# First projection of layer 0 begun on half of scale and shift; each pair's scatter tied behind the next pair's last up product

## The chip, the cores and the metric

The program runs on one core of a Trainium2 chip. The metric is the device time of one execution in microseconds; the time of a kernel is the median of several runs. The engines named below are TensorE (PE, its weight loads PEld), VectorE (DVE), ScalarE (ACT), GpSimd (POOL) and SyncE (SP), whose queue issues nearly all weight transfers.

## The reference

Two layers of a streaming encoder, 256 frames of 1024 features, in float32. Every sub-layer normalises x, multiplies by 1 + scale and adds shift; scale, shift and a gate come from a conditioning vector c by a matrix product.

```
c_act = silu(c)
sh1, sc1, g1, sh2, sc2, g2 = split(c_act @ w_mod[layer] + b_mod[layer], 6)
h = rmsnorm(x, norm_g) * (1 + sc1) + sh1
layer 0:  q, k, v, f = split(h @ w_in)            # 1024, 1024, 1024, 16 columns
          cum = cumsum(log_sigmoid(f + b_f));  scores = q k / 8 + cum_t - cum_s, causal softmax
layer 1:  latent attention on a shared k/v made from layer 0's output
x = x + g1 * (attention(h) @ w_o)
h = rmsnorm(x, ffn_norm_g) * (1 + sc2) + sh2
x = x + g2 * sum over 16 experts of  combine_e * ((silu(h Wg_e) * (h Wu_e)) Wd_e)   # 2 experts of a frame
out = rmsnorm(x, final_norm_g)
```

## The kernel before

**Weights.** All weights flow through one planned list, `stream`. `plan` appends a piece of mostly 1 MB (L91), `issue` (L238) starts its transfer from SP's queue as soon as one of the ten ring buffers `w` (or a named spare buffer) is free, and `done`/`drop` (L275 to L288) free it and issue the next. The list's order is the order of arrival: the four pieces of scale `sc1_0`, the four of shift `sh1_0` (L185), the forget-gate columns `wf` (L187), and then the twelve pieces of `w_in` (four head groups g, each q, k and v, L189), each followed by one piece of another modulation vector (`g1_0`, `sc2_0`, `sh2_0`; `weave`, L174).

**Modulation.** `mods` (L302) multiplies such pieces with c: those named in `ONPE` on PE (L321), into PSUM bank 6, the others on DVE (L327, L329), two instructions a piece, tied behind the last instruction of the first `turn` (`state["turned"]`). When all four pieces are in, `fin_col` (L457) brings the vector into columns: for `sc1_0` and `sh1_0` by 32 small products each (L464), then two DVE additions (L468, L470).

**Start of layer 0.** x is normalised to `xn`, `turn` (L548) transposes it on PE with feature k of every eighth column together, `leave` (L566) applies scale and shift on the way out of PSUM and splits the result into a high and a low part (`h2`). Every product of this part is three fp32r products (`mm3`, L521: high by high, high by low, low by high); weights are split likewise by `split` (L498), the high part on ACT (L517), the low part on POOL or DVE (L518). The f product (L1075 to L1080) stands first; its result goes through a chain on DVE and ACT (L1083 to L1088) into two rows of q and k. `proj_a` (L1090) makes q, k and v of one head group, 48 products each; `attention` (L643) runs the groups and puts scores, softmax and the value products between them.

**Experts.** `moe` (L747) gathers frames per expert into 64 slots with one-hot products (`fetch`, L869) and walks eight pairs of experts (L976): 64 recorded products for gate and up (`wide`, L899), SiLU (L985), `act` = silu(gate) * up * weight on DVE (L996), transposes of it (L1003), copies `aT` (L1006, L1007), 32 products down in two column halves (L1018), and `yb`, `yh` (L1031 to L1034) as the scaled result. `scatter(i - 1)` (L907, L911) adds the previous pair's `yh` into the output rows in PSUM by eight products; `slots(i + 1)` (L880) makes the next pair's one-hot matrix. Pair OV = 4 is special: its branch for overflowing experts stands behind its gate products, with scatter(3) ahead of it. The last pair scatters half by half (L1044).

**Order.** Every engine runs its instructions in a fixed order. That order is not that of the program text: a planner, which simulates the program on a time line of its own, orders each engine's queue when the kernel is built. `tc.issue_after(x)` forbids it to put the instructions inside ahead of x. So scatter(i - 1), written behind up of pair i (L997), stands for most pairs between the gate products of pair i.

Of the kernel before, what the change touches and what calls it, by code (L numbers as in the profile page):

```python
# [22 lines left out]
F32 = mybir.dt.float32  # L23
# [4 lines left out]
ALU = mybir.AluOpType  # L28
# [18 lines left out]
ONPE = ('sc1_0', 'sh1_0', 'sc2_0', 'sh_kv', 'sh1_1', 'g2_0', 'sc2_1', 'g2_1')  # L47
# [26 lines left out]
def trunk_kernel(ctx, tc, A, out):  # L74
# [217 lines left out]
    nc.gpsimd.memset(bcast, 0.0)  # L292

# [8 lines left out]
    def mods():  # L302
        while state["used"] < len(stream) and stream[state["used"]][0][0] == "mod":
# [5 lines left out]
            if j == 0:  # L309
                macc[name] = bank(MB)[:, 0:256] if name in ONPE else big.tile([128, D], F32, name="macc", bufs=2)  # L310
# [5 lines left out]
            for kk in range(2):  # L316
                k = 2 * j + kk
                if name in ONPE:
                    with later(name, j):
                        for q in range(4):  # L320
                            PE.matmul(acc[32 * q:32 * q + 32, :], cact[:, k:k + 1].to_broadcast([128, 32]),  # L321
                                      w[:, kk, 256 * q:256 * q + 256], start=k == 0, stop=k == 7)
# [9 lines left out]
            if j == 3:  # L332
# [124 lines left out]
    def fin_col(name, bias, gain=None):  # L457
        rows = mod_rows(name)
        r_ = cst.tile([128, 8], F32, name="c_" + name)
        if name in ("sc1_0", "sh1_0"):  # L460
            at = bank(MB)[:, 0:8]
            for k in range(8):
                for q in range(4):
                    PE.matmul(at[32 * q:32 * q + 32, k:k + 1], rows[:, k::8], pick[:, q:q + 1], start=True, stop=True)  # L464
        else:
            nc.gpsimd.dma_start(r_, rows[0:128:32, :].rearrange("p (j k) -> p j k", k=8))
            at = r_
        V.tensor_tensor(r_, at, bias, op=ALU.add)  # L468
# [278 lines left out]
    def moe(l, G, sh, acc):  # L747
# [143 lines left out]
        def wide(nm, i, b):  # L891
            ps = bank(b)
            for c, (k0, nk) in enumerate(wide_rows(nm, l, i)):
# [7 lines left out]
                if i == 0 and nm == "g":  # L901
                    after[5] = last
                for e in range(2):
                    done((nm, l, i, c, e))
            return ps

# [69 lines left out]
        for i in range(E // 2):  # L976
# [20 lines left out]
            if i and i != OV:  # L997
                scatter(i - 1)
# [13 lines left out]
            for p, (c0, n) in enumerate(cols):  # L1012
# [15 lines left out]
                if p == 0 and i < E // 2 - 1:  # L1028
                    slots(i + 1, 5)
# [25 lines left out]
    finish_at["sc1_0"] = lambda: fin_col("sc1_0", bcol[0][:, 1, :], pk("ga"))  # L1055
    finish_at["sh1_0"] = lambda: fin_col("sh1_0", bcol[0][:, 0, :])
# [14 lines left out]
    turn(xn, 8, 8, [(h2p, M["sc1_0"], M["sh1_0"], True)], (0, 1, 2, 3))  # L1071
    state["turned"] = state["left"]

    pf = bank(6)
    for c in range(2):  # L1075
        wfs = split(get("wf")[:, 4 * c:4 * c + 4, :], "wf")
        for kk in range(4):
            k = 4 * c + kk
            mm3(pf[0:96, 0:256], [w_[:, kk, :] for w_ in wfs], [h2[:, j, k, :] for j in range(2)], k == 0, k == 7)
    done("wf")  # L1080
# [9 lines left out]
    def proj_a(g, part, qkv):  # L1090
        if part == 0:
# [6 lines left out]
            for j, dst, scl in ((0, qa, HD ** -0.5), (1, ka, 1.0)):  # L1098
                ps = ring_bank()
# [10 lines left out]
            return qa, ka, v  # L1110
        ps = ring_bank().rearrange("p (t n) -> p t n", t=T)
# [278 lines left out]
```

## Time and profile before

| | |
|---|---|
| time, three runs | 857.45 us median (856.47 to 857.65) |
| profiled execution, its own time | 856.38 us |
| its span in the trace | 854.3 us |
| busy in the span | PE 767.0 (90%), DVE 376.0 (44%), ACT 266.6 (31%), POOL 166.2 (19%) |
| transfers | 296.32 MB, mean 347 GB/s; SP's queue 90.8% of 16 DMA engines' span |

The 2.1 us between span and time lie outside the trace. Layer 0's attention runs from the start to 187 us, its experts to 450, layer 1's attention to 600, its experts to the end.

### The profile page before, as it was taken

What the parts mean: (1) busy time and instruction counts of PE and PEld (TensorE: products, weight loads), DVE (VectorE), ACT (ScalarE), POOL (GpSimd) and SP (SyncE); (2) the same over time, 40 slices, a digit from 0 to 9 for tenths busy, and PEclk for the clock granted to TensorE, in tenths of its full rate; (3) what the DMA queues carried; (4) which work ended last, traced back from release to release, by engine and by line L of the source; (5) the groups of instructions that cost most, each with busy time, mean ns of one, the idle gap of its engine ahead of it and who ended that gap; (6) DMA issues with size and microseconds to landing.
All of it is one profiled execution on the core that took longest, in us unless ns stands there. A gap on an engine that the chain in (4) does not pass through costs nothing.

```text
span 854.3 us, 11932 instructions
## 1 busy us (share of the span) xinstructions
PE 767.0 (90%) x4522; PEld 441.9 (52%) x4522; DVE 376.0 (44%) x831; ACT 266.6 (31%) x578; POOL 166.2 (19%) x151
## 2 busy tenths in 40 slices
PE   4678999998999999899978798999799999999994
PEld 2477888765344343243327666777533534434332
DVE  2389599977112211221238949665712321122112
ACT  2346456534101011010127555765511110111002
POOL 1273567320000000000007755321100000000000
PEclk9699999999999999999998999999799999999998
DMA  9997897899999999999997769768789999999992
GB/s 347 383 376 272 275 347 261 315 380 392 414 397 394 417 402 403 418 407 403 414 397 270 231 226 362 293 222 273 269 292 402 402 374 413 367 393 398 402 392 82
DMA packets 102855, 296.32 MB, mean 347 GB/s; under 512 B 6992, under 2 KB 26624, under 8 KB 90496
## 3 DMA queue, kind: packets, MB, share of 16 engines
q1 hardware_dynamic: 101968, 293.79, 90.8%
q10 hardware_dynamic: 288, 1.05, 0.3%
q8 instruction: 39, 0.64, 0.3%
q0 software_dynamic: 528, 0.59, 0.2%
q14 instruction: 32, 0.26, 0.1%
HBM read 294.30 MB, written 1.05 MB: 346 GB/s over the span
## 4 chain that ended last, share of the span: by engine, by line
issue 28%; PE 23%; DVE 5%; DMA 2%; ACT 1%; POOLq 0%; POOL 0%; SPq 0%; another core or an unknown queue 0%; DVEq 0%; ACTq 0%
PE b L899 6%; PE b L1018 4%; PE b L522 2%; PE b L523 2%; PE b L524 2%; DVE macc L329 1%; DMA fg<-in_final_norm_g_dram 1%; PE b L911 1%; PE b L631 1%; DMA w<-in_w_mod_dram 1%; DVE wl L518 1%; DMA w<-in_exp_w_gate_dram 1%; PE b L321 1%; PE b L557 1%; PE b L593 1%
## 5 line engine op out<-in xcount | busy, mean ns | idle before, releaser
L899 PE MATMUL b<-w,XG 128*64 128x512 f32 x1024 | 239.0, 595 | 0.6 <-PEq L917 0.6
L518 POOL TENSOR_TENSOR wl<-w,wh 128x512 fp32r<-128x512 f32 (+3 forms) x90 | 132.4, 1487 | 354.0 <-ACT wh L517 350.5
L899 PEld LDWEIGHTS b<-w,XG 128*64 128x64 f32 x1024 | 78.2, 137 | 140.8 <-issue 135.3
L1018 PE MATMUL b<-w,aT 128*64 128x512 f32 (+1 forms) x528 | 125.8, 585 | 3.7 <-ACT aT L1006 3.7
L996 DVE SCALAR_TENSOR_TENSOR act<-sg,rcs,b 128x512 f32<-128x512 f32 x16 | 12.0, 747 | 211.3 <-PE b L899 211.3
L517 ACT ACTIVATE wh<-w 128x512 fp32r<-128x512 f32 (+3 forms) x136 | 76.6, 587 | 63.3 <-PE b L524 22.7
L1018 PEld LDWEIGHTS b<-w,aT 128*64 128x64 f32 x528 | 38.2, 136 | 66.0 <-issue 56.2
L329 DVE SCALAR_TENSOR_TENSOR macc<-w,cact,macc 128x1024 f32<-128x1024 f32 x42 | 63.6, 1513 | 1.2 <-DMA w<-in_w_mod_dram 0.7
L1033 ACT ACTIVATE yh<-yb 128x512 fp32r<-128x512 f32 x31 | 19.6, 631 | 113.2 <-DVE yb L1031 113.2
L518 DVE TENSOR_TENSOR wl<-w,wh 128x512 fp32r<-128x512 f32 (+2 forms) x46 | 44.3, 973 | 19.8 <-ACT wh L517 19.7
L1031 DVE TENSOR_TENSOR yb<-b,g 128x512 f32<-128x512 f32 (+1 forms) x33 | 22.2, 674 | 64.1 <-PE b L1018 64.1
L985 ACT ACTIVATE sg<-b 128x512 f32<-128x512 f32 x16 | 9.6, 598 | 119.9 <-PE b L899 119.9
L539 POOL TENSOR_TENSOR rs<-rs,mhalf 128x1 f32<-128x1 f32 (+1 forms) x9 | 5.4, 602 | 206.6 <-DVE rs L538 206.6
L321 PE MATMUL b<-w,cact 128*32 128x256 f32 x512 | 39.9, 418 | 6.0 <-DMA w<-in_w_mod_dram 5.7
L524 PE MATMUL b<-h,wl 128*128 128x256 f32 (+1 forms) x136 | 40.5, 299 | 4.7 <-DVE wl L518 4.3
L522 PE MATMUL b<-h,wh 128*128 128x256 f32 (+1 forms) x136 | 40.3, 300 | 3.5 <-ACT h L579 3.5
L1006 ACT ACTIVATE aT<-b 128x256 f32<-128x256 f32 x16 | 6.1, 384 | 117.1 <-PE b L1003 117.1
L869 PEld LDWEIGHTS b<-P,xs 128*128 128x128 f32 x256 | 34.4, 203 | 15.2 <-DVE XG L875 6.5
L869 PE MATMUL b<-P,xs 128*128 128x256 f32 x256 | 39.3, 304 | 1.6 <-DVE P L834 1.6
L523 PE MATMUL b<-h,wh 128*128 128x256 f32 (+1 forms) x136 | 39.5, 292 | 0.0
L911 PE MATMUL b<-yh,PT 128*128 128x512 f32 x112 | 34.4, 422 | 2.1 <-ACT yh L1033 2.1
L523 PE MATMUL b<-wl,h 128*128 128x256 f32 (+1 forms) x96 | 30.0, 316 | 2.9 <-POOL wl L518 2.4
(296 smaller groups left out, 1208.8 us busy)
## 6 DMA issues: line engine op xcount, KB each, us to landing
w<-in_exp_w_down_dram SPq DMA_DIRECT2D x50, 1024.0 KB, 12.5
w<-in_w_mod_dram SPq DMA_DIRECT2D x48, 1024.0 KB, 8.9
w<-in_exp_w_gate_dram SPq DMA_DIRECT2D x48, 1024.0 KB, 12.8
w<-in_exp_w_up_dram SPq DMA_DIRECT2D x48, 1024.0 KB, 13.0
w<-in_a_w_in_dram SPq DMA_DIRECT2D x12, 1024.0 KB, 12.4
w<-in_exp_w_gate_dram SPq DMA_DIRECT2D x42, 256.0 KB, 7.2
w<-in_exp_w_up_dram SPq DMA_DIRECT2D x40, 256.0 KB, 5.9
w<-in_kv_w_mod_dram SPq DMA_DIRECT2D x8, 1024.0 KB, 7.0
```

Source lines behind the costliest of these rows:

```text
L321: PE.matmul(acc[32 * q:32 * q + 32, :], cact[:, k:k + 1].to_broadcast([128, 32]), w[:, kk, 256 * q:256 * q + 256], start=k == 0, stop=k == 7)
L329: V.scalar_tensor_tensor(acc, w[:, kk, :], cact[:, k:k + 1], acc, op0=ALU.mult, op1=ALU.add)
L517: SC.activation(hi, src, AF.Copy)
L518: lo_eng.tensor_tensor(lo, src, hi.bitcast(F32), op=ALU.subtract)
L522: PE.matmul(ps, l[0], r_[0], start=start, stop=False)
L523: PE.matmul(ps, l[0], r_[1], start=False, stop=False)
L524: PE.matmul(ps, l[1], r_[0], start=False, stop=stop)
L869: at = PE.matmul(ps[:, 256 * kk:256 * kk + 256], xs[n % 2, n // 2][:, 128 * k:128 * k + 128], P[g][:, n // 2].rearrange("p e s -> p (e s)" ...
L899: last = PE.matmul(ps[64 * e:64 * e + 64, :], XG[i // 2, k // 4][:, k % 4, o:o + 64], ws[e][:, kk, :], start=k == 0, stop=k == 7).ins
L911: PE.matmul(acc[t, half], PT[i][:, t, :], yh[:, j, 512 * half:512 * half + 512], start=False, stop=False)
L1018: at = PE.matmul(py[64 * e:64 * e + 64, 0:n], aT[:, k, 64 * e:64 * e + 64], ws[e][:, k, :], start=k == 0, stop=k == 3).ins
L1031: V.tensor_tensor(yb[:, 0:n], py[:, 0:n], M[f"g2_{l}"][:, cs_], op=ALU.mult)
```

## The change

There are two parts. In the first, scale and shift of the first sub-layer are fetched and finished in halves of 512 features (`sc1_0a`, `sh1_0a`, then `sc1_0b`, `sh1_0b`), in two 1 MB pieces each. h2 is made in two halves (`turn_half`), with 128 neighbouring features in a block; w_in and wf are read in the matching order, q, k and v of group 0 and wf in half pieces (0.5 MB, wf 0.2 MB) that stand between the second half's modulation pieces. The products of the first half of the features (`half_qk`, `half_v`, `half_f`) are written ahead of the second half's `turn_half(1)`; the sums stay open in PSUM banks 4, 5, 7 and 0. `fin_half` replaces `fin_col` for these vectors: bias and gain are laid out by rows beforehand (`halfrows`, three small DMAs on POOL's queue, in a `macc` buffer), and one product with `pick` turns the row into columns. In the second part, scatter(i - 1) is tied behind the last up product of pair i; in pairs 0 and 4, which have no scatter there, slots(i + 1) takes that place.

```diff
-ONPE = ('sc1_0', 'sh1_0', 'sc2_0', 'sh_kv', 'sh1_1', 'g2_0', 'sc2_1', 'g2_1')
+HALVES = ('sc1_0a', 'sh1_0a', 'sc1_0b', 'sh1_0b')
+ONPE = HALVES + ('sc2_0', 'sh_kv', 'sh1_1', 'g2_0', 'sc2_1', 'g2_1')
...
-    for it in mod_unit("sc1_0", W0, D) + mod_unit("sh1_0", W0, 0):
+    def mod_half(name, c0):
+        r = W0.rearrange("(p k) n -> p k n", k=8)
+        return [(("mod", name, j), r[:, 4 * j:4 * j + 4, c0:c0 + D // 2]) for j in range(2)]
+
+    win = A["a_w_in"][0].rearrange("(k p) n -> p k n", p=128)
+    wff = A["w_f"].rearrange("p (k n) -> (p k) n", k=8).rearrange("(k p) n -> p k n", p=128)
+    def in_half(j, c):
+        return ("in", 0, j, c), win[:, 4 * c:4 * c + 4, j * D:j * D + 256]
+    scb, shb = mod_half("sc1_0b", D + D // 2), mod_half("sh1_0b", D // 2)
+    for it in (mod_half("sc1_0a", D) + mod_half("sh1_0a", 0)
+               + [in_half(0, 0), scb[0], in_half(1, 0), scb[1], shb[0], in_half(2, 0), shb[1], (("wf", 0), wff[:, 0:4]),
+                  (("wf", 1), wff[:, 4:8])]):
         plan(*it)
-    plan("wf", A["w_f"].rearrange("p (k n) -> p k n", k=8))
-    win = A["a_w_in"][0].rearrange("(p k) n -> p k n", k=8)
-    main = [(("in", g, j), win[:, :, j * D + 256 * g:j * D + 256 * g + 256]) for g in range(4) for j in range(3)]
+    main = [in_half(j, 1) for j in range(3)]
+    main += [(("in", g, j), win[:, :, j * D + 256 * g:j * D + 256 * g + 256]) for g in range(1, 4) for j in range(3)]
...
+    def fin_half(name, c, gain):
+        rows = wk.tile([128, 128], F32, name="mrows", tag="t2", bufs=3)
+        V.tensor_tensor(rows, macc.pop(name), halfrows[:, 2 * gain + c], op=ALU.add)
+        if gain:
+            V.scalar_tensor_tensor(rows, rows, 1.0, halfrows[:, 4 + c], op0=ALU.add, op1=ALU.mult)
+        ps = bank(MB)[:, 0:4]
+        PE.matmul(ps, rows, pick, start=True, stop=True)
+        M[name] = cst.tile([128, 4], F32, name="c_" + name)
+        V.tensor_copy(M[name], ps)
...
-            if i and i != OV:
-                scatter(i - 1)
+            with tc.issue_after(ends["u"]):
+                if i in (0, OV):
+                    slots(i + 1, 7)
+                else:
+                    scatter(i - 1)
...
-                if p == 0 and i < E // 2 - 1:
+                if p == 0 and i < E // 2 - 1 and i not in (0, OV):
                     slots(i + 1, 5)
...
-    turn(xn, 8, 8, [(h2p, M["sc1_0"], M["sh1_0"], True)], (0, 1, 2, 3))
-    state["turned"] = state["left"]
+    turn_half(0)
+    half_qk(0, 0)
+    half_qk(1, 0)
+    half_v(0)
+    half_f(0)
+    turn_half(1)
+    state["turned"] = state["left"]
+    half_f(1)
...
+                if g == 0:
+                    half_qk(j, 1)
+                    head_rows(sums[j], dst, scl)
+                    continue
...
+        if g == 0:
+            SC.activation(qkv[2], half_v(1), AF.Copy)
+            return
```

`half_qk(j, c)`, `half_v(c)` and `half_f(c)` run the same `split` and `mm3` calls as before over the four feature blocks of half c, 24, 24 and 12 products, and end with `done` of their piece.

## Rows read from the trace of the kernel before

**Rows 1.** Busy us of each engine (instructions), clock, DMA share, GB/s, of four stretches
```profile
20.00:36.00 16.00, 8.41 (x148) 3.56 (x141) 3.08 (x9) 4.51 (x10) 2.48 (x2) 0.56 1.05 388
36.00:67.00 31.00, 24.57 (x171) 23.29 (x172) 27.39 (x28) 13.48 (x22) 19.26 (x13) 0.90 1.06 378
67.00:187.00 120.00, 112.15 (x817) 95.45 (x815) 101.08 (x203) 63.53 (x153) 61.19 (x40) 0.99 0.85 302
80.00:180.00 100.00, 92.83 (x690) 79.33 (x690) 84.95 (x167) 54.64 (x130) 56.01 (x36) 0.99 0.83 293
```

**Rows 2.** Time line of the start: start us, us, engine, line [idle before <-releaser]
```profile
28.84 1.93 PE L321 MATMUL b<-w,cact 128*32 128x256 f32 x16 [0.63 <-DMA w<-in_w_mod_dram]
35.89 0.74 PE L522 MATMUL b<-h,wh 128*96 128x256 f32 x2 [3.45 <-ACT h L579]
```

**Rows 3.** DMA view, 20 to 30 us: GB/s of 40 slices
```profile
GB/s 426 410 442 360 426 393 410 442 393 426 377 475 344 410 410 393 410 361 426 459 377 410 410 442 377 389 471 348 393 381 389 385 344 365 356 352 356 344 352 352
```

**Rows 4.** DMA view, 187 to 437 us: GB/s of 40 slices
```profile
GB/s 407 397 362 412 392 420 424 418 386 395 399 385 407 394 393 421 418 421 390 392 423 422 415 384 395 422 419 420 387 398 421 419 417 387 403 422 419 411 387 396
```

**Rows 5.** Time line of PE, 46 to 68 us
```profile
46.81 0.39 PE L524 MATMUL b<-h,wl 128*128 128x256 f32 x1 [0.85 <-DVE wl L518]
...
56.27 0.58 PE L524 MATMUL b<-h,wl 128*128 128x256 f32 x1 [3.15 <-DVE wl L518]
...
66.63 0.49 PE L592 MATMUL b<-ka,qa 96*128 96x128 f32 x2 [1.85 <-DVE ka L715]
...
67.86 0.47 PE L522 MATMUL b<-h,wh 128*128 128x256 f32 x1
```

**Rows 6.** Time line of DVE: rows of group 1's qa and ka
```profile
62.64 1.93 DVE L1093 TENSOR_SCALAR qa<-zef,fA,fB 32x1024 f32<-32x1024 f32 x1
64.49 1.37 DVE L1097 TENSOR_SCALAR ka<-zef,fMA,fMB 32x256 f32<-32x256 f32 x4
```

**Rows 7.** Busy us of PE (instructions), 138.3 to 144.5 us
```profile
138.30:144.50 6.20, 6.20 (x53) 1.00 0.69 245
```

**Rows 8.** Waits of PE, layer 0's experts: us in total, times, longest
```profile
PE b L1003 <- DVE act L996: 6.5, 7, 0.9
PE b L911 <- ACT yh L1033: 2.1, 2, 1.4
```

**Rows 9.** Waits of PE, layer 1's experts
```profile
PE b L1003 <- DVE act L996: 4.6, 5, 0.9
```

**Rows 10.** Time line of PE, layer 0's experts: pairs 1, 4 and 7
```profile
253.79 2.13 PE L911 MATMUL b<-yh,PT 128*128 128x512 f32 x8
...
351.13 1.46 PE L911 MATMUL b<-yh,PT 128*128 128x512 f32 x4 [0.63 <-ACT yh L1033]
...
357.62 1.46 PE L911 MATMUL b<-yh,PT 128*128 128x512 f32 x4 [1.44 <-ACT yh L1033]
...
434.47 4.50 PE L1018 MATMUL b<-w,aT 128*64 128x512 f32 x18 [0.54 <-ACT aT L1006]
439.67 1.46 PE L1044 MATMUL b<-yh,PT 128*128 128x512 f32 x4 [0.69 <-ACT yh L1033]
441.05 3.65 PE L1018 MATMUL b<-w,aT 128*64 128x512 f32 x14
```

**Rows 11.** Issue of layer 0's last down piece (SP's time line)
```profile
423.61 2.55 SPq L250 DMA_DIRECT2D w<-in_exp_w_down_dram  x1
```

**Rows 12.** The same piece in the DMA view: KB, us to landing
```profile
w<-in_exp_w_down_dram SPq DMA_DIRECT2D x1, 1024.0 KB, 14.2
```

**Rows 13.** Issue of layer 1's last down piece
```profile
828.20 0.54 SPq L250 DMA_DIRECT2D w<-in_exp_w_down_dram  x1
```

**Rows 14.** The same piece in the DMA view
```profile
w<-in_exp_w_down_dram SPq DMA_DIRECT2D x1, 512.0 KB, 8.1
```

**Rows 15.** Time line of PE: layer 1's last down products
```profile
833.79 7.11 PE L1018 MATMUL b<-w,aT 128*64 128x512 f32 x48 [0.53 <-ACT aT L1006]
```

**Rows 16.** DMA view, 811 to 829 us: packets of pieces of 0.5 MB
```profile
DMA packets 2120, 7.25 MB, mean 403 GB/s; under 512 B 143, under 2 KB 250, under 8 KB 1754
```

More of the change, by code (lines that the diff above doesn't have):

```diff
@@ L315, in mods @@
             acc = macc[name]
-            for kk in range(2):
-                k = 2 * j + kk
+            nk, n = (4, 128) if name in HALVES else (2, 256)
+            for kk in range(nk):
+                k = nk * j + kk
                 if name in ONPE:
@@ L459, in fin_col @@
         r_ = cst.tile([128, 8], F32, name="c_" + name)
[L460 to L468, printed above, removed]
+        nc.gpsimd.dma_start(r_, rows[0:128:32, :].rearrange("p (j k) -> p j k", k=8))
+        V.tensor_tensor(r_, r_, bias, op=ALU.add)
         if gain is not None:
@@ L902, in wide @@
                     after[5] = last
+                ends[nm] = last
                 for e in range(2):
@@ L905, in wide @@
             return ps
+        ends = {}
         def scatter(i):
@@ L1052, in moe @@
                         gains(half, acc)
-    finish_at["sc1_0"] = lambda: fin_col("sc1_0", bcol[0][:, 1, :], pk("ga"))
-    finish_at["sh1_0"] = lambda: fin_col("sh1_0", bcol[0][:, 0, :])
+    for c, nm in enumerate("ab"):
+        finish_at["sc1_0" + nm] = lambda nm=nm, c=c: fin_half("sc1_0" + nm, c, 1)
+        finish_at["sh1_0" + nm] = lambda nm=nm, c=c: fin_half("sh1_0" + nm, c, 0)
     finish_at["g1_0"] = lambda: fin_bc("g1_0", "g1")
@@ L1070, in trunk_kernel, with turn_half @@
     h2, h2p = parts("h2")
[L1071 to L1076 removed]
+    sums = {}
+    def turn_half(c):
+        for i in range(2):
+            ps = bank(2 * c + i)
+            for kk in range(2):
+                k = 4 * c + 2 * i + kk
+                for t in range(T):
+                    PE.transpose(ps[:, 256 * kk + 128 * t:256 * kk + 128 * t + 128], xn[:, t, 128 * k:128 * k + 128], ident)
+            leave({2 * i: ps.rearrange("p (a b) -> p a b", a=2)}, 2 * i, h2p[2 * c:2 * c + 2],
+                  M["sc1_0" + "ab"[c]], M["sh1_0" + "ab"[c]], True)
@@ L1077, in trunk_kernel, with half_f, half_qk @@
+    def half_f(c):
+        if c == 0:
+            sums["f"] = bank(0)
+        w = get(("wf", c))
+        wfs = split(w, "wf")
         for kk in range(4):
             k = 4 * c + kk
-            mm3(pf[0:96, 0:256], [w_[:, kk, :] for w_ in wfs], [h2[:, j, k, :] for j in range(2)], k == 0, k == 7)
-    done("wf")
+            mm3(sums["f"][0:96, 0:256], [w_[:, kk, :] for w_ in wfs], [h2[:, j, k, :] for j in range(2)], k == 0, k == 7)
+        done(("wf", c))
+    def half_qk(j, c):
+        if c == 0:
+            sums[j] = bank(4 + j)
+        w = get(("in", 0, j, c))
+        for blk in range(2):
+            ws = split(w[:, :, 128 * blk:128 * blk + 128], "in")
+            for kk in range(4):
+                k = 4 * c + kk
+                mm3(sums[j][:, 256 * blk:256 * blk + 256], [w_[:, kk, :] for w_ in ws],
+                    [h2[:, i, k, :] for i in range(2)], k == 0 and blk == 0, k == 7 and blk == 1)
+        done(("in", 0, j, c))
@@ new lines, in half_v @@
+    def half_v(c):
+        if c == 0:
+            sums[2] = bank(7)
+        ps = sums[2].rearrange("p (t n) -> p t n", t=T)
+        w = get(("in", 0, 2, c))
+        for cc in range(2):
+            ws = split(w[:, 2 * cc:2 * cc + 2, :], "inv")
+            for kk in range(2):
+                k = 4 * c + 2 * cc + kk
+                for t in range(T):
+                    mm3(ps[:, t], [h2[:, i, k, 128 * t:128 * t + 128] for i in range(2)],
+                        [w_[:, kk, :] for w_ in ws], k == 0 and t == 0, k == 7 and t == T - 1)
+        done(("in", 0, 2, c))
+        return ps
```

15 lines of the change are left out of this document (12 added, 3 removed).

## The prediction

> **What bounds the kernel now.** I read the table by stretches first, then the time line of the start, then PE's waits among the experts, and last when the final weights land there.
>
> The start is bound by transfers. Up to 36 us DMA is full, while PE does little but modulation, at a mean clock of 0.56, which is mostly the 1.2 GHz level [rows 1]. The last shift piece lands at about 28.8 us, and the first projection product runs at 35.9, after h2 [rows 2]. From 36 to 67 us DMA is still full, yet PE waits more for VectorE than for data: 0.85, 3.15 and 1.85 us [rows 1, 5]. From 67 to 187 us PE is busy 112.15 of 120 us and VectorE 101.08, while DMA has slack: 0.83 from 80 to 180 us, or 17 us unused [rows 1]. In layer 0's experts two things are nearly equal. PE's waits are few: seven times 0.93 us for `act`, twice for `yh` (2.1 us together) [rows 8]. But DMA delivers about 390 GB/s in the down pieces (2 KB a packet) and 420 in gate and up without a break [rows 4], and the last down piece, issued at 423.61 and 14.2 us under way, lands at 437.8 [rows 11, 12]. PE starts the first column half at 434.47; its 18 products take 4.50 us, so the second half, two of them, begins at about 438.1 [rows 10]. The lead is 0.3 us. In layer 1 the last piece lands at 828.20 + 8.1 = 836.3 [rows 13, 14]; its products are the last quarter of 7.11 us from 833.79 and begin at about 839.1 [rows 15], a lead of 2.8 us.
>
> **The change part by part.**
>
> *Arrival at the start.* In front of the second shift half now stand 8.4 MB of modulation in 2 KB packets and three halves of w_in, 1.6 MB. At about 390 instead of 410 GB/s [rows 3, 4] the former cost 21.5 instead of 20.5 us, +1.0. The latter cost 4.5 us at 352 GB/s, the end of [rows 3]. So the first shift half, 4.2 MB, is in about 10 us before all of it was, near 18 us, and the second near 34.3 instead of 28.8. wf goes from 128 packets to 1024 of 384 bytes: 1.0 us before, now from 1.0 (its bytes at 410 GB/s) to 3.0 (the time that 1024 packets of 1 KB take at 352). I take 2.0, +1.0, between the two since no such packet is in the rows. Everything behind, group 1's first piece included, lands 1 to 3 us later.
>
> *Work moved.* 24 + 24 + 24 + 12 = 84 products of group 0 and f no longer need the second half. 53 products take 6.20 us, 0.117 each [rows 7], so 84 are worth 9.8 us of PE. They can run from about 22 us on, where PE is idle for half of the time [rows 1]. At the lower clock they would take twice as long and run to about 43, which is still ahead of the last half piece of group 0: 34.3 + 2 for wf + 3 x 1.5 + 2 x 2.55 of modulation between them = 45.9. Gone are `fin_col`'s 64 small products, on the path at the start only; `fin_half`'s one product, two or three VectorE steps for each half are not more. `halfrows`' DMAs have some 15 us to land; POOL, whose queue issues them, is busy 2.48 of 16 us even at 20 to 36 [rows 1].
>
> *What is late next.* PE begins group 1's products at 67.86 [rows 5]. Group 1's q piece landed near 28.8 + 1.0 + 4 x 3.0 (w_in, 1 MB at 352 GB/s) + 3 x 2.55 (modulation at 410) = 49.5 us; 1 to 3 us later and with a split ahead it can be used at 51.5 to 54, so arrival bounds the gain at 14 to 16. PE's own work gives 9.8. VectorE gives less: it was busy 27.39 of 31 us from 36 to 67 [rows 1]. It must do all of this again but for group 1's rows (1.93 + 1.37 [rows 6]) and about 1.5 us of the first half's h2, so it needs 22.6 us and can be at the same place 8.4 us earlier. Bounds 0 and 14; I take 9, near these two. From 67 us on nothing is removed and PE's load over the stretch stays near nine tenths, so the 9 us last to 187. Transfers can follow, as 17 us of them were idle; the buffers of the attention come free 9 us earlier, and so does the unbroken stream of the experts.
>
> *Scatter behind up, layer 0.* Where the scatter stood there already, L1003 follows without a wait: pair 1, eight products, 2.13 us [rows 10], more than the 0.93 that `act` takes. Five more pairs (2, 3, 5, 6, 7) gain 0.93 each, 4.65 us. Pair 4's own scatter no longer waits for `yh`: 2.07 [rows 10]. Pairs 0 and 4 only move the slots' two products from one side of the transposes to the other, 0. Together 6.7 us on PE, but the last down piece lands 0.3 us before its use, relative to a stream that moves by the 9. After it come 16 products (3.65 us) and one scatter half (1.46) [rows 10]: 437.8 + 5.1 = 442.9 against 441.05 + 3.65 = 444.7 before. That gives 1.8; with the scatter half fitted in while PE waits it is 3.3, and with an up piece also late about 0. I take 1.8.
>
> The wait added is on PE's queue. Behind the scatter stand the pair's transposes and its down products. They had waited for `act` anyway; `yh` is rewritten only after those, so no one else waits.
>
> *Layer 1.* PE waits five times for `act` [rows 9]: four (2, 5, 6, 7) go, 3.7 us, pair 4 keeps its sum. The last piece's lead of 2.8 us caps this at 2.8.
>
> *Sum.* 9 + 1.8 + 2.8 = 13.6 us off the profiled execution's 856.38 gives 842.8. The median of the runs is 1.07 above that execution, so 844.
>
> **Small pieces.** The change cuts 3.1 MB of w_in into pieces of 0.5 MB. [Rows 16] hold the last expert pair, whose eight pieces of 0.5 MB are among transfers that run at 403 GB/s, as fast as whole ones, with a full queue. That they lose speed is the second rival below. The Trainium skill ("DMA: Bandwidth & Descriptors", Bandwidth) asks for at least 1 MiB a transfer to reach three quarters of the peak; here the trace does not bear that out for pieces in a full queue.
>
> **The rivals.**
>
> *Start's gain lost on the way (849 to 855).* VectorE has 101 of 120 us of work after 67 us, in a fixed order that the planner writes anew. If group 0 finished early only leaves it waiting for the same softmax steps, the 9 us shrink to 0 to 3. Only the expert gains of 4.6 are left: 856.38 - 4.6 + 1.07 = 852.9. For it speaks VectorE's share; against it, that PE was busier. Chance 0.17.
>
> *Small pieces stream at half their rate.* Then the w_in halves take 17.6 instead of 8.8 us, group 1's piece is in near 61 instead of 52, and its bound on the gain falls from 14 to 6: 844 + 3 = 847. Chance 0.04.
>
> *The tie does nothing.* If transfers, not PE, already set the end of both expert stages, the 4.6 us are not gained: 848.5. [Rows 10] and the leads above bear it out for most of layer 0, not for layer 1. Chance 0.07.
>
> *Slower: VectorE's modulation products start later.* `g1_0`'s first piece landed at about 28.8 + 1.0 + 3.0 + 2.55 = 35.4. Now it is behind the second shift half, wf and a half piece: 34.3 + 2 + 1.5 + 2.6 = 40.4, 5 us later. If VectorE, not PE, is the bound from there on and its order is not made denser, attention ends 5 us later, layer 0's transfers shift with it and their 1.8 is lost, and layer 1's 2.8 stays: 857.45 + 5 - 2.8 = 859.7. It decides if VectorE's idle 19 us of the 120 cannot be used. A new order by the planner can carry it to 866. Against it: VectorE also has less to wait for at 46 to 67 us. Chance 0.12.
>
> **How the numbers follow.** The forecast, 844, has 0.60, in 838 to 849: the start's term from 4 to 14 with the experts' from 2 to 6. The range leaves out the slower case and the best tail: 835 to 856. A difference under 0.2%, 1.7 us, is about what cannot be told from no change. Faster than that is the forecast, the first three rivals: 0.60 + 0.17 + 0.04 + 0.07 = 0.88, less 0.05 of the first rival's edge near 855.7: 0.83. Same: that edge and a piece of the slower case, 0.06. Slower 0.11.
>
> **What would show it.** First projection products at 21 to 24 us with few gaps to 38, second shift half's products near 34; group 1's first product at 55 to 61 instead of 67.86; attention's end at 175 to 180. Among the experts, L911 of every pair but 4 directly ahead of L1003, no `act` wait in pairs 1 to 3 and 5 to 7, no L911 waiting for `yh`, and new short waits of L899 or L1018 for exp_w pieces in pairs 6 and 7. It is wrong if PE reaches group 1 no earlier, or if layer 0's experts end less than 8 us earlier.

## The result, and the profile after

The changed kernel takes 847.97 us (median of 4 runs, 846.11 to 850.46) beside 857.55 us of the kernel before (4 runs); the ratio is 0.9877 [0.9859, 0.9895]. In a second comparison it was 0.9874 [0.9846, 0.9901]. The forecast was 844 in 835 to 856. The size fits; the places do not. The profiled execution took 847.37 us with a span of 845.2, 9.1 under the 854.3 of before, and this is where these went. The marks are starts of rows in the two traces (us): the first score product of layer 0, the first expert product of a layer (gate), and the last copy of layer 0's output x out of PSUM, which ends its experts.

```
                               before   after    difference in the stage
f's first step on VectorE       46.79   54.24
first scores                    66.63   71.84
first gate product, layer 0    208.62  208.87    start and attention  +0.25   (forecast -9)
last x copy, layer 0           448.02  447.34    experts              -0.93   (forecast -1.8)
first gate product, layer 1    622.21  617.08    layer 1's attention  -4.45   (forecast  0)
end of the last instruction    849.68  840.37    experts and output   -4.18   (forecast -2.8)
```

A second trace of the changed kernel (after_again, below) has 211.40, 448.55, 619.34 and 843.44 us for the last four marks. One kernel's marks differ by up to 3 us between executions, so the first two stage differences of the table tell no change from none; the last two have the same sign in both traces (-3.4 and -3.4 in the second).

The stretches of [rows 1], for the kernel after (busy us of PE, PEld, DVE, ACT, POOL with their instructions, granted clock, DMA share, GB/s):

```profile
20.00:36.00 16.00, 10.53 (x123) 8.68 (x116) 3.40 (x6) 5.39 (x10) 6.18 (x5) 0.68 1.08 366
36.00:67.00 31.00, 26.33 (x239) 24.62 (x239) 22.34 (x25) 15.69 (x26) 16.51 (x12) 0.91 1.06 379
67.00:187.00 120.00, 110.71 (x798) 93.49 (x797) 103.96 (x215) 61.91 (x152) 61.05 (x40) 0.98 0.86 311
```

PE does 2.1 us more in the first stretch and 1.8 more in the second than before, and from 67 to 187 us 1.4 less. A good part of the products did run early: counted in the two time lines, PE has started 84 products of group 0 and f by 43 us, beside 47 before, and it comes to group 1's first one at 58.72 us instead of 67.86. Yet the first scores start 5.2 us later than before. The time line of PE shows the order (start, us, engine, line, idle before, releaser):

```profile
18.79 1.95 PE L343 MATMUL b<-w,cact 128*32 128x128 f32 x64 [0.26 <-DVE c_sc_0a L497]
21.15 0.39 PE L495 MATMUL b<-pick,mrows 128*128 128x4 f32 x2 [0.41 <-DVE mrows L491]
23.27 1.60 PE L343 MATMUL b<-w,cact 128*32 128x128 f32 x32 [1.73 <-DMA w<-in_w_mod_dram]
28.20 1.50 PE L343 MATMUL b<-w,cact 128*32 128x128 f32 x22 [3.33 <-DMA w<-in_w_mod_dram]
29.63 0.80 PE L548 MATMUL b<-h,wh 128*128 128x256 f32 x2
...
42.96 1.95 PE L343 MATMUL b<-w,cact 128*32 128x128 f32 x64
47.88 0.53 PE L548 MATMUL b<-h,wh 128*96 128x256 f32 x1 [2.16 <-ACT h L605]
...
58.72 0.28 PE L548 MATMUL b<-h,wh 128*128 128x256 f32 x1
...
71.84 0.49 PE L618 MATMUL b<-ka,qa 96*128 96x128 f32 x2 [1.46 <-DVE ka L1179]
```

The first half's shift is ready at 21.5 us, as forecast. The first projection product runs at 29.63. Two queues hold it until then. PE's has the second scale half's products in front, and these wait 1.73 and 3.33 us for their transfer. ScalarE's has the k half's split (`wh`) ahead of the first half's `hf`; the split waits for its transfer until 25.46, so the first high part of h2 is there only at 29.1, the end of the first of the two rows at 28.48:

```profile
20.43 1.15 ACT L543 ACTIVATE wh<-w 128x512 fp32r<-128x512 f32 x2 [12.45 <-DMA w<-in_a_w_in_dram]
25.46 1.15 ACT L543 ACTIVATE wh<-w 128x512 fp32r<-128x512 f32 x2 [3.88 <-DMA w<-in_a_w_in_dram]
26.52 1.00 ACT L603 ACTIVATE hf<-b,c_sh_0a,c_sc_0a 128x256 f32<-128x256 f32 x2
28.48 1.15 ACT L605 ACTIVATE h<-hf 128x512 fp32r<-128x512 f32 x2 [0.96 <-DVE hf L597]
```

The second shift half lands at 35.2; its products stand behind the first halves of q, k, v and f and run at 42.96, so h2's second half comes at 47.9.

Then f's chain, which leads from the f product to two rows of q and k. On VectorE of the kernel after, its four steps (L1165, L1166, L1169, the scan L1170) stand among the products for the gate vector `g1_0` (L349, L351):

```profile
48.46 1.78 DVE L349 TENSOR_SCALAR macc<-w,cact 128x1024 f32<-128x1024 f32 x1
50.28 3.93 DVE L351 SCALAR_TENSOR_TENSOR macc<-w,cact,macc 128x1024 f32<-128x1024 f32 x3
54.24 0.48 DVE L1165 TENSOR_SCALAR zef<-b,pack 32x256 f32<-32x256 f32 x1
...
55.84 2.32 DVE L351 SCALAR_TENSOR_TENSOR macc<-w,cact,macc 128x1024 f32<-128x1024 f32 x1
58.19 1.41 DVE L1166 SCALAR_TENSOR_TENSOR zef<-zef 32x256 f32<-32x256 f32 x1
...
62.26 0.42 DVE L1169 SCALAR_TENSOR_TENSOR zef<-zef 32x256 f32<-32x256 f32 x1
62.71 2.19 DVE L351 SCALAR_TENSOR_TENSOR macc<-w,cact,macc 128x1024 f32<-128x1024 f32 x1
64.93 1.67 DVE L1170 TENSOR_TENSOR_SCAN zef<-ones,zef 32x256 f32<-32x256 f32 x1
```

The scan ends at 66.6 us; before it ended at 54.6. Group 0's scores need the rows that VectorE makes from it, and their first product waits for those (`ka`, at 71.84). By group 1's scores the 9.1 us of lead are 0.9 (95.24 for 96.14).

Among layer 0's experts PE's waits now read so, for [rows 8]; the last lines are the tail of [rows 10]:

```profile
PE b L925 <- DMA w<-in_exp_w_up_dram: 5.6, 5, 1.4
PE b L925 <- DMA w<-in_exp_w_gate_dram: 4.4, 4, 1.3
PE b L1076 <- ACT yh L1065: 2.8, 2, 2.1
PE b L1050 <- ACT aT L1038: 2.2, 5, 0.5
PE b L1035 <- DVE act L1025: 1.1, 2, 0.5
...
438.21 0.73 PE L1076 MATMUL b<-yh,PT 128*128 128x512 f32 x2 [0.69 <-ACT yh L1065]
438.87 2.79 PE L1050 MATMUL b<-w,aT 128*64 128x512 f32 x10
...
445.47 1.46 PE L1076 MATMUL b<-yh,PT 128*128 128x512 f32 x4 [2.13 <-ACT yh L1065]
```

The seven waits for `act` are two (pairs 0 and 4), `yh` inside the stage is gone, and in their place stand 10.0 us of waits for gate and up pieces, in pairs 5 and 7 (0.2 us in pair 6). The last down piece lands at 437.0 instead of 437.8. Layer 1's last pair, for [rows 15]: a scatter half (L1076) fills the time until the last down piece, which lands at 831.7 instead of 836.3:

```profile
825.60 5.81 PE L1050 MATMUL b<-w,aT 128*64 128x512 f32 x34 [0.53 <-ACT aT L1038]
831.34 1.30 PE L1076 MATMUL b<-yh,PT 128*128 128x512 f32 x4
832.57 1.94 PE L1050 MATMUL b<-w,aT 128*64 128x256 f32 x14
834.44 1.78 PE L1076 MATMUL b<-yb,PT 128*128 128x256 f32 x7
```

Before, that scatter half stood behind the last down products, and the last scatter waited once more:

```profile
840.83 1.20 PE L1044 MATMUL b<-yh,PT 128*128 128x512 f32 x4
843.68 2.06 PE L1044 MATMUL b<-yb,PT 128*128 128x256 f32 x8 [1.65 <-DVE yb L1031]
```

### The profile page after: what moved, and what is told of

The parts are those of the page before. It is cut to its first block, busy times and chain, and to the rows that moved or that the text cites. A ratio compares the mean times of both kernels' runs of the same rounds, so it can differ in the third digit from the quotient of the medians.

```text
span 845.2 us, 11973 instructions
## 1 busy us (share of the span) xinstructions
PE 759.6 (90%) x4530; PEld 454.3 (54%) x4530; DVE 374.7 (44%) x838; ACT 265.5 (31%) x576; POOL 169.5 (20%) x155
## 4 chain that ended last, share of the span: by engine, by line
issue 22%; PE 21%; DVE 8%; DMA 8%; ACT 2%; SPq 0%; POOLq 0%; POOL 0%; another core or an unknown queue 0%; ACTq 0%; DVEq 0%
DMA w<-in_exp_w_up_dram 7%; PE b L925 5%; PE b L1050 3%; PE b L548 2%; DVE macc L351 2%; PE b L549 2%; PE b L550 2%; PE b L895 1%; DVE wl L544 1%; DMA fg<-in_final_norm_g_dram 1%; PE b L940 1%; PE b L657 1%; PE b L343 1%; PE b L643 1%; PE b L619 1%
## 5 line engine op out<-in xcount | busy, mean ns | idle before, releaser
L925 PE MATMUL b<-w,XG 128*64 128x512 f32 x1024 | 234.3, 595 | 15.5 <-DMA w<-in_exp_w_up_dram 6.9
L925 PEld LDWEIGHTS b<-w,XG 128*64 128x64 f32 x1024 | 80.7, 137 | 156.1 <-issue 125.5
L1050 PE MATMUL b<-w,aT 128*64 128x512 f32 (+1 forms) x528 | 121.8, 586 | 4.0 <-ACT aT L1038 4.0
L351 DVE SCALAR_TENSOR_TENSOR macc<-w,cact,macc 128x1024 f32<-128x1024 f32 x42 | 68.6, 1633 | 0.4
L544 DVE TENSOR_TENSOR wl<-w,wh 128x512 fp32r<-128x512 f32 (+2 forms) x46 | 39.4, 864 | 20.4 <-ACT wh L543 20.3
L343 PE MATMUL b<-w,cact 128*32 128x256 f32 (+1 forms) x640 | 40.0, 368 | 6.2 <-DMA w<-in_w_mod_dram 6.0
L548 PE MATMUL b<-h,wh 128*128 128x256 f32 (+1 forms) x136 | 41.1, 307 | 3.0 <-ACT h L605 2.2
L549 PE MATMUL b<-h,wh 128*128 128x256 f32 (+1 forms) x136 | 40.9, 302 | 0.0
L901 DVE TENSOR_SCALAR XG<-b,c_sc,c_sh 128x256 f32<-128x256 f32 x32 | 17.4, 543 | 36.6 <-ACT XG L903 36.4
L903 ACT ACTIVATE XG<-b,c_sh,c_sc 128x256 f32<-128x256 f32 x32 | 17.9, 560 | 46.9 <-PE b L895 46.9
```

The lines of the kernel that those rows point to most:

```text
L351: V.scalar_tensor_tensor(acc, w[:, kk, :], cact[:, k:k + 1], acc, op0=ALU.mult, op1=ALU.add)
L544: lo_eng.tensor_tensor(lo, src, hi.bitcast(F32), op=ALU.subtract)
L548: PE.matmul(ps, l[0], r_[0], start=start, stop=False)
L549: PE.matmul(ps, l[0], r_[1], start=False, stop=False)
L925: last = PE.matmul(ps[64 * e:64 * e + 64, :], XG[i // 2, k // 4][:, k % 4, o:o + 64], ws[e][:, kk, :], start=k == 0, stop=k == 7).ins
L1050: at = PE.matmul(py[64 * e:64 * e + 64, 0:n], aT[:, k, 64 * e:64 * e + 64], ws[e][:, k, :], start=k == 0, stop=k == 3).ins
```

## The experiments

Each was run beside the kernel before, in the same rounds; that kernel's own times went from 855 to 863 us there, so ratios are given, and a difference inside the intervals is not read. The marks are starts of rows (the last: an end) in the one profiled execution (us):

```
              first    first gate  last x copy  first gate   end of
              scores   layer 0     layer 0      layer 1      last     ratio to before
tie_only       66.84    210.26      448.68       622.87      845.09   0.9886 [0.9857, 0.9916]
halves_only    71.01    208.18      448.11       619.05      847.65   0.9968 [0.9949, 0.9987]
less_before    66.57    210.10      441.05       614.95      847.71   0.9956 [0.9933, 0.9979]
less_dma       70.51    210.74      434.93       605.36      830.03   0.9704 [0.9671, 0.9737]
f_first        70.51    202.81      445.39       615.61      838.75   0.9854 [0.9820, 0.9887]
f_early        65.67    209.96      449.39       621.19      844.45   0.9868 [0.9840, 0.9895]
f_lead         63.85    206.22      444.99       616.79      840.39   0.9837 [0.9815, 0.9859]
late_mod       71.30    205.75      438.47       632.45      856.91   1.0044 [1.0026, 1.0062]
late_lead      63.33    203.80      435.77       630.93      854.79   1.0009 [0.9989, 1.0029]
tie_uq         67.03    208.91      448.73       618.31      840.79   0.9871 [0.9852, 0.9890]
after_again    71.19    211.40      448.55       619.34      843.44   0.9874 [0.9846, 0.9901]
f_lead_2       63.61    205.80      444.96       615.22      839.57   0.9835 [0.9810, 0.9861]
```

**Each part alone.** tie_only has the diff's lines in `wide`, at the scatter and at `slots`, and the old start; halves_only has the rest.

> The kernel before with the change's second part alone: scatter and slots stand behind the pair's last up product, the start is the old one. Theory A (the start's halves give nothing, what the change gains it gains in layer 1, and layer 0's experts are held by transfers): layer 0's x copy ends 0 to 1 us earlier than in the kernel before (448.0), its experts now wait for exp_w pieces; layer 1's experts are 4.2 us shorter, as between the two traces (622.21 to 849.68 before, 617.08 to 840.37 after). Whether layer 1's attention is also 3.7 us shorter tells whose that gain is: 853 without it, 849.5 with it. Theory B (the halves carry the gain of layer 0 and of layer 1's attention): only the 4.2 us of layer 1's experts, 853.3, and layer 0 unchanged.

> The changed kernel without its second part: the start with halves, scatter and slots as before. Theory A: the first gate product of layer 0 comes near 208.9 as in both traces, layer 0 ends near 448, layer 1's experts take the old 227.5 us; 857 if layer 1's attention is not shortened by this part, 853.5 if it is. Theory B (the start's gain is there and is used further on): 850 to 853, with the layer-0 experts beginning at least 3 us earlier than 208.6.

The tie carries most: 0.9886 alone, 0.9968 for the halves, 0.9877 for both. tie_only's layer-1 experts take 222.2 us instead of 227.5, its layer-0 experts 238.4 instead of 239.4, with 9.7 us of waits for pieces. The halves leave layer 0's experts where they were (first gate 208.18, last x copy 448.11), as theory A had it, and shorten layer 1's attention: from last x copy to first gate 170.9 us instead of 174.2. tie_only as it was profiled (851.76 us, the longest but one of its six) has 174.2 there.

**Do transfers hold layer 0's experts?** less_dma takes twelve 1 MB pieces away from the changed kernel, less_before from the old one. Both experts of a pair then multiply with the even one's up weights, so the results are not those of the reference, and PE's work is the same:

```diff
+    def shared(name):
+        return name[0] == "u" and name[1] == 0 and name[2] >= 2 and name[4] == 1
...
+                ws[1] = ws[0] if ws[1] is None else ws[1]
```

> The changed kernel, with the odd expert's up weights of layer 0's pairs 2 to 7 not loaded: both experts of a pair multiply with the even one's. PE's work is unchanged, 12 pieces of 1 MB are not moved (some 30 us of transfer at 410 GB/s). Theory A (transfers hold layer 0's experts once the tie is in): PE's waits for exp_w pieces and the late yh, 12.8 us together in the trace of the changed kernel between 349 and 427 us, go, less what act waits come back; the x copy ends 7 to 12 us earlier than 447.3, and the whole is 836 to 841. Theory B (PE's own chain act, yh, scatter holds it, and the transfer waits only stand where other waits would): the x copy ends within 2 us of 447.3, the whole is 846 to 848.

> The kernel before, with the odd expert's up weights of layer 0's pairs 2 to 7 not loaded, as in less_dma: both experts of a pair multiply with the even one's. Theory A (without the tie PE's waits for act and yh hold layer 0's experts and transfers are only just covered): the x copy ends within 3 us of 448.0, and the whole is 854 to 858, so that the tie is worth 10 us and more in layer 0 where transfers don't hold it. Theory B (transfers held it already before the change): it ends at 441 or earlier, 843 to 850.

The leading waits of PE in layer 0's experts, those for `aT` (2.2 and 1.9 us) left out, less_dma first, then less_before:

```profile
PE b L1088 <- ACT yh L1077: 2.7, 1, 2.7
PE b L1047 <- DVE act L1037: 1.1, 2, 0.5
```

```profile
PE b L1015 <- DVE act L1008: 6.4, 7, 0.9
PE b L1056 <- ACT yh L1045: 2.7, 1, 2.7
```

With 12 pieces less every wait for a piece is gone, and the stage (first gate to last x copy) takes 224.2 us instead of 238.5: theory A, by more than it said. In the old kernel the same cut brings it from 239.4 to 230.95. So both theories on less_before are half wrong (A had its time, B its x copy): the old stage is 8 us longer with the pieces, though its list of waits names only `act` and `yh`. The traces show where. Between the transposes (L1003) of pairs 3 and 6 PE takes 95.3 us before and 87.9 in less_before. PE's order is another there: the two waits of pair 4's scatter for `yh` (2.07 us) are gone, and from pair 5 to pair 6 the same 143 products are recorded as 31.97 us of busy time before, in shorter runs of each kind, and as 29.96 in less_before, both at a clock of 1.00. That the planner chose the older order because pieces come late is likely, but was not tested. Between the two kernels without those pieces the stage differs by 6.8 us. That is what the tie is worth to PE in layer 0 where transfers do not bind; where they do, 0.9 is left of it in this trace (2.2 in after_again). (less_before loses 5 us again in layer 1's experts, 232.8 instead of 227.5; this was not followed up.)

**The start in another order.** f_first loads wf ahead of the v half and turns the second half of h2 behind the k half (the lists are shortened here):

```diff
-[in_half(0, 0), scb[0], in_half(1, 0), scb[1], shb[0], in_half(2, 0), shb[1], wf0, wf1]
+[in_half(0, 0), scb[0], in_half(1, 0), scb[1], shb[0], shb[1], wf0, wf1, in_half(2, 0)]
```

> The changed kernel with another order at the start: the two halves of wf are loaded right behind the second shift half, ahead of the v half of w_in; the second half of h2 is turned right behind the k half, f's products follow, and the v half's come after the scan. Nothing is left out. Theory A (f's chain came 7.5 us later because the second half of modulation stood behind the v half in the queues of PE, and wf behind it in the stream, and that ate the start's gain): the second shift half's products run at 34 to 37 us instead of 43 to 45, f's first chain step at 42 to 46 instead of 54.2, the first scores at 62 to 66 instead of 71.8, and layer 0's experts begin 3 to 6 us before 208.9; 842 to 845. Theory B (VectorE's load from 46 to 187 us takes the gain whatever the order): the marks up to the first scores come earlier, but the first gate product stays within 1.5 us of 208.9; 847 to 849.

f's first step came at 52.94, not 42 to 46: the planner again set the second shift half's products (landed at 32.9) behind the first halves', at about 41. The first gate product came 6 us earlier, which theory A had (3 to 6), but not by its way: the first scores came only 1.3 us earlier, and at 150 us the lead is 1.0 us (150.10 for 151.13). The other 5 arise behind that: PE's wait of 2.73 us for `c_sh` at 175 and that of 2.25 for `rmask` at 202 are gone, and the clock from 165 to 190 us is 1.00 instead of 0.93. Of the 6 us the last x copy shows 1.95. f_early puts both halves of wf ahead of the k half as well; f_lead adds two ties (f's first half, `half_f(0)`, stands behind `last_mod` too):

```diff
+    with tc.issue_after(last_mod):       # last product of the second shift half
+        half_qk(1, 0)
+        half_v(0)
-    state["turned"] = state["left"]      # VectorE's gate products behind h2's second half
+    state["turned"] = V.tensor_tensor_scan(...).ins
```

> The changed kernel with the start's stream in another order: q half of w_in, second scale and shift halves, both wf halves, then k and v halves; f's products are written ahead of the first k and v halves. Nothing is left out. Theory A (what stands ahead of f's products in the stream and in PE's queue made the scan late): f's first chain step at 43 to 48 us instead of 54.2, first scores at 62 to 67, first gate product of layer 0 at 198 to 203; yet the x copy of layer 0 ends only 2 to 4 us earlier than 447.3, since transfers hold the experts: 843 to 846. Theory B (VectorE's own products decide the scan's end): f's first step comes earlier but the scan still ends at 63 to 66; first scores at 69 to 71; 845 to 848.

> The kernel of f_early with two ties more: the first k and v halves and f's first half stand behind the last product of the second shift half's modulation, and VectorE's products for the first gate stand behind the scan. Nothing is left out. Theory A: f's first step at 40 to 44 us, scan's end at 47 to 52, first scores at 60 to 64, first gate product of layer 0 at 196 to 201, and still the x copy ends only 2 to 5 us earlier than 447.3, because the last weights' landing (437.0) moves by no more: 842 to 846. Theory C (once the attention ends earlier the whole stream of transfers and the experts follow one for one): the x copy ends 8 us or more earlier, 836 to 840. Against both: the gate's products come late on VectorE and hold buffers, then the attention ends no earlier than 208.

f_early: f's first step at 52.43, scan's end at 61.8; no gain that times can tell from the changed kernel. f_lead, VectorE again:

```profile
47.01 0.48 DVE L1165 TENSOR_SCALAR zef<-b,pack 32x256 f32<-32x256 f32 x1 [2.62 <-PE b L550]
47.53 0.83 DVE L1166 SCALAR_TENSOR_TENSOR zef<-zef 32x256 f32<-32x256 f32 x1
...
51.66 0.42 DVE L1169 SCALAR_TENSOR_TENSOR zef<-zef 32x256 f32<-32x256 f32 x1 [1.55 <-ACT zef L1168]
...
52.82 1.39 DVE L1170 TENSOR_TENSOR_SCAN zef<-ones,zef 32x256 f32<-32x256 f32 x1
54.24 1.63 DVE L349 TENSOR_SCALAR macc<-w,cact 128x1024 f32<-128x1024 f32 x1
```

The scan ends at 54.2, 12 us earlier than in the changed kernel; the first scores come 8 us earlier, the first gate product 2.7, the last x copy 2.35. So the scan's place was the loss up to the first scores; at the first gate product it gives back 2.7 of the 9 us. Group 1's scores are still 9.1 us earlier than in the changed kernel (86.13 for 95.24), group 2's only 1.9 (119.75 for 121.63): VectorE has the gate's products to make up there (busy 30.7 us of the 33 from 67 to 100, 25.7 in the changed kernel). Theory C (one for one) is out. f_lead takes 1.6% less than the kernel before, and was run once more against scatter:

> The kernel of f_lead once more, to see whether its 0.9837 holds against the changed kernel's 0.9874 and 0.9877. If the scan's earlier end is worth what the traces show (x copy of layer 0 2.4 us earlier than in the changed kernel, 0.3%), the ratio is 0.982 to 0.986; if the difference was scatter between executions, 0.986 to 0.990.

0.9835 [0.9810, 0.9861]: the same (its first gate at 205.80, last x copy at 444.96). It is the best of this study, 0.4% under the changed kernel, with intervals that just touch. The changed kernel was run again as well:

> The changed kernel once more, on the chip and in the rounds of the next two, so that they can be compared with it: ratio 0.986 to 0.990 to the kernel before, as measured (0.9877).

0.9874 [0.9846, 0.9901].

**Bytes moved behind layer 0.** late_mod is the changed kernel, late_lead is f_lead, each with

```diff
-            + mod_unit("sc1_1", W1, D) + mod_unit("sh1_1", W1, 0))
...
     plan_moe(0, mod_unit("g2_0", W0, 5 * D))
+    for it in mod_unit("sc1_1", W1, D) + mod_unit("sh1_1", W1, 0):
+        plan(*it)
```

> The changed kernel with 8.4 MB moved in the stream: layer 1's first scale and shift pieces of w_mod stand behind layer 0's last down piece instead of ahead of its experts. All the same work is done, nothing is left out. Theory A (what is to be moved up to the last down piece sets the end of layer 0's experts): 8.4 MB are 20.6 us at 406 GB/s, more than PE's waits for pieces there and the late yh (12.8), so the x copy ends 8 to 12 us earlier than 447.3, near the 434.9 of the kernel with 12 pieces not loaded; layer 1's first steps wait at most 1 to 4 us for the late shift; 836 to 841. Theory B (the experts follow PE and the attention's end, and the waits for pieces only stand where others would): x copy within 2 us of 447.3, layer 1 waits for its modulation, 848 to 856.

> The kernel of f_lead (f's products and scan first) with the same 8.4 MB moved behind layer 0's last down piece. Theory A: with transfers out of the way layer 0's experts follow the attention's end, so that the earlier first gate product is worth its full size: x copy ends as many us ahead of that of late_mod as its first gate product comes ahead (1 to 4), 833 to 840. Theory C (the start's gain is lost all the same, by PE's own order in the experts' first pair): no difference to late_mod beyond 1 us.

Theory A holds for layer 0, and its time is wrong by 25 us. The last down piece lands at 427.3 instead of 437.0 and the last x copy starts at 438.47 instead of 447.34; late_lead's is 2.7 earlier still, with a first gate product 1.95 earlier, so there the start's gain comes through. But layer 1 then waits. From the last x copy to the first step that takes keys (`ka`) out of PSUM, late_mod and then after:

```profile
438.50:502.80 64.30, 41.07 (x253) 33.19 (x254) 39.94 (x65) 27.91 (x61) 30.63 (x27) 0.76 0.82 298
```

```profile
447.30:488.80 41.50, 33.14 (x185) 27.29 (x186) 38.63 (x55) 26.06 (x59) 32.02 (x24) 0.92 0.70 254
```

It takes 64.3 instead of 41.5 us, and PE's waits there are led by these two:

```profile
PE b L549 <- ACT h L606: 7.2, 1, 7.2
PE b L584 <- DVE xn L572: 6.7, 1, 6.7
```

The moved pieces land until 448.6, and the weights behind them 12 us later than in the changed kernel (the first kv_w_down piece 450.1 for 438.5), while layer 1 begins 9 us earlier. The clock is 0.76 in this stretch (0.92 after). The 9 us saved in layer 0 cost 23.

**Layer 1's attention.** In the kernel after, group 1's query products run from 514.9 us, ahead of most of the second scale's modulation; before, the modulation stands in front of them (517.1 to 519.7). The largest block of it, before and then after:

```profile
518.30 1.50 PE L321 MATMUL b<-w,cact 128*32 128x256 f32 x24
```

```profile
521.33 1.91 PE L343 MATMUL b<-w,cact 128*32 128x256 f32 x26
```

No line of the diff names that stage; the planner wrote its order anew. PE's longest wait behind it does not tell the two apart (2.19 us for `yatt` at 532 before, 2.18 for `macc` at 533 after). tie_uq is tie_only with the modulation behind those queries:

```diff
     def later(name, j):
+        if name == "sc2_1" and 0 < j < 4:
+            return tc.issue_after(state["uq"])   # last query product of the group
```

> The kernel with the tie alone, and one thing more: in layer 1's attention three of the four pieces of the second scale's modulation products (24 of 32) are tied behind the last query product of group 1, as the changed kernel has them by its planner; nothing is left out. Theory A (the 3.3 to 4.5 us that layer 1's attention gains in the four kernels with halves come from this order: group 1's query products ahead of the modulation): the first gate product of layer 1 comes 167 to 168.5 us after layer 1's first transposes instead of 171.5, and the time is 3 to 4 us under that of the tie alone, 845 to 846. Theory B (they come from something else that the halves bring): 171 to 172 us, and 848.5 to 850.

From first transposes to first gate product layer 1's attention takes 171.46 us before, 171.17 in less_before and 171.46 in tie_only; 167.01 after, 166.85 in tie_uq, 167.5 to 169.1 in the seven other runs with halves and the old place of these pieces. In the traces theory A holds. The clock is not the reason: tie_uq's stage had 0.93 and is still 4.3 to 4.6 us shorter than those of less_before and before, which have the old order at 0.94 and 0.95. (tie_only's had 0.91, so a part of its distance may be the clock's; those of after and the seven others had 0.93 to 0.96.) The times do not show it: 848.40 us, where A said 845 to 846 and B 848.5 to 850, and 0.9871 [0.9852, 0.9890] beside 0.9886 [0.9857, 0.9916] of tie_only, whose trace is of a long execution. So the order is worth 3 to 4 us in the traces, and what it gives to the median is not shown.

## Why the prediction was right or wrong

**The start's term failed, behind the place where it was taken.** "I take 9, near these two" was right at that place: PE came to group 1 at 58.72 us, 9.1 earlier, inside the forecast 55 to 61. On the way "They can run from about 22 us on, where PE is idle for half of the time" did not hold, since the products were free of the second half in the data but not in the queues of PE and ScalarE, and the first ran at 29.63; the idle time that followed was enough all the same. The step that failed is "so the 9 us last to 187". Of the 9.1 us, 0.9 are left at group 1's scores and -0.25 at the first gate product (group 3's scores, 146.04 for 149.08, had 3.0). PE's load was as forecast (110.71 of 120 us from 67 to 187). VectorE's part was not: it "can be at the same place 8.4 us earlier" counted its work and not its order. h2's second half came at 47.9 us, the gate's products, some 1.3 us each, came ahead of f's steps and between them, the scan ended 12.0 us later, and the scores started 5.2 us later. f_lead shows that this order was the cause up to the scores: with it put right the scan ends where it did before and the scores come 2.8 us earlier than before. It also shows that this is not the whole loss: PE comes to group 1 at 55.14 there, and the first gate product is only 2.4 us earlier than before.

**"Transfers can follow, as 17 us of them were idle" failed by itself.** From 180 to 440 us DMA is full in both kernels (share 1.03, 405 GB/s, before and after), so with every piece loaded the end of layer 0's experts can move only by what has landed up to 180 us. Before, then f_lead, from 0 to 180 us, and before from 180 to 440:

```profile
DMA packets 25589, 58.21 MB, mean 323 GB/s; under 512 B 1354, under 2 KB 13786, under 8 KB 25574
```

```profile
DMA packets 29366, 59.40 MB, mean 330 GB/s; under 512 B 2601, under 2 KB 15041, under 8 KB 29350
```

```profile
180.00:440.00 260.00, 245.01 (x1281) 106.36 (x1280) 66.86 (x165) 41.20 (x76) 5.68 (x8) 1.00 1.03 405
```

A MB more up to 180 us is worth 1 / 0.405 = 2.5 us of landing. In the ten traces that load every piece in the planned place:

```
              MB landed    last down piece     the same from before's   last x copy
              by 180 us    of layer 0 landed   437.8 and the MB alone   behind it
before          58.21          437.8                437.8                 10.3
after           58.53          437.0                437.0                 10.3
after_again     58.14          438.3                437.9                 10.3
tie_only        58.00          438.5                438.3                 10.2
tie_uq          58.01          438.2                438.3                 10.5
halves_only     58.84          437.0                436.2                 11.1
f_first         59.24          435.1                435.2                 10.3
f_early         57.65          438.9                439.1                 10.5
f_lead          59.40          434.4                434.8                 10.6
f_lead_2        59.54          434.7                434.5                 10.2
```

The landing follows the bytes within 0.8 us, and the x copy follows the landing, the old kernel included. So f_first's attention, 6 us shorter, moved the copy by 1.95.

**Layer 0's experts.** PE's 6.7 us were right (6.8 without the pieces), and so was it that the landing caps them: 0.9 for 1.8, which one trace does not tell apart. The waits come in pairs 5 and 7, not 6 and 7.

**Layer 1's experts.** 4.2 us for 2.8. "The last piece's lead of 2.8 us caps this" holds for the start of the last products alone, and left out what lies behind them. The landing is at the same place of the stage as before (214.6 us behind its first gate product, 214.1 before), and the last products start 1.4 us earlier in it. The rest comes from the scatter half, which PE now runs while it waits for the piece (831.34) and no longer behind it (840.83, 1.20 us), and from the wait of 1.65 us for `yb`, which is gone. For layer 0 the prediction had such a case ("with the scatter half fitted in"), for layer 1 it had not. tie_only bears this out: its last piece lands at 836.5, as late as before's 836.3, and its experts end 4.6 us earlier:

```profile
836.07 1.29 PE L1050 MATMUL b<-yh,PT 128*128 128x512 f32 x4
837.29 1.94 PE L1024 MATMUL b<-w,aT 128*64 128x256 f32 x14
839.16 1.99 PE L1050 MATMUL b<-yb,PT 128*128 128x256 f32 x8
```

**Not in the sum:** 4.45 us in layer 1's attention (3.4 in after_again), in traces that show an order which no line of the change asks for.

**The rivals.** "Start's gain lost on the way" is what happened: group 0 was finished early, PE was ahead at group 1, and no gain was left at 208 us. VectorE's order did it, for the most part by f's chain ahead of the first scores and not by softmax steps. Such steps behind the scores are seen in f_lead, where 9.1 us on the changed kernel shrink to 1.9 within one group. The rival's 852.9 was missed because of layer 1. "Slower: VectorE's modulation products start later" had its premise: they began at 48.46 instead of 38.19. Its consequence did not follow. In f_lead they begin at 54.24, and the attention ends earlier than in either kernel. "Small pieces at half rate": the first half of shift was there at 21.5 and the second landed at 35.2 for 34.3 forecast; no. "The tie does nothing" is refuted by tie_only.

By its own last sentence the prediction was wrong: PE reached group 1 as early as it said, but layer 0's experts ended 0.7 us earlier, not 8. That 847.97 lies near the forecast, in its 838 to 849, is luck: 5.8 us come from layer 1 that it did not have there (4.45, and 1.4 above the experts' term). Without them it would be some 853.8, inside the whole range but near the rival's 852.9.

## What to carry to other kernels

Work that no longer needs a late input runs early only if every engine's queue has it ahead of what still waits: read the queue's order for each engine that it passes, and tie the chain that others need (here f's scan) ahead of bulk work. A lead of one engine is a gain only once the next thing that it waits for is early too. Before adding up gains of stages, look whether a full stretch of transfers lies behind them; then only bytes loaded earlier, or fewer bytes, move its end, and a list of waits that names other engines does not exclude it. Bytes put behind one stage were paid here at the start of the next (9 us saved, 23 lost), which had no slack of its own. When a landing caps a stage, look also at what stands behind the last products: it can be moved into the wait.

## What the runs showed that was not expected

The time of one kernel on one core moves with its mean granted clock: of 17 runs of the kernel before, three at 0.970 took 855.4 to 856.9 us, and ten at 0.963 and 0.964 took 858.5 to 860.4. Marks of single profiled executions are to be compared with this 0.4% in mind. The two halves of wf, in packets of 384 bytes, took 1.3 us from the landing in front of them (35.2 us) to their own (36.5): 0.39 MB at about 295 GB/s, beside 405 to 410 of the large pieces and the 2.0 us that the prediction took.
